# Keeping the residual rows of a small hybrid network unscaled between its blocks, with both norm factors from one chain of roots

## The chip, the cores and the metric
One core of a Trainium2 chip runs one program. Its engines are TensorE (PE in the profile, with its weight loads as PEld), VectorE (DVE), ScalarE (ACT), GpSimd (POOL) and SyncE (SP, which here only issues transfers). The metric is device time in microseconds (us); lower is better. Quoted times are the median of several runs, and a trace is one profiled execution.

## The reference, cut to what matters
The network takes x of 512 tokens by 1024 features through a first block and two hybrid layers. The first block ends in a residual sum and a norm, and its result is both the residual and, after one more norm, the input of the first layer:

```python
x = x + jnp.einsum('bse,ed->bsd', y, w_out[layer])
return _rmsnorm(x, final_norm_g)              # end of the first block
...
h = rms_norm(x, norm1_g)                      # start of a hybrid layer
...
x = x + merged.astype(dt) @ w_out
h2 = rms_norm(x, norm2_g)                     # then the feed-forward part
```

With s the unnormed sum, the first norm is s times r1 times gf1 (r1 a factor per token, gf1 a gain per feature). The second norm needs the squares of that product.

## The kernel before, in words
Activations lie feature-major: eight tiles [128 features, 512 tokens]. Every product is made of three float32r matmuls (`mm3`, lines 387 to 391: high by high, low by high, high by low). A weight chunk is loaded by SP (line 376), its high part is cast by ACT (line 382) or, each fourth, by DVE (line 380), and its low part is the difference, on DVE (line 383). Two buffers each of the raw, high and low chunk rotate. A chunk is one projection of 24 matmuls with 512 columns (`proj`), or a third of a token-major product (`proj_tm`, lines 420 to 422, tiles named pt).

The framework orders the instructions of each engine ahead of time, by its own estimate of their times (`schedule_with_timeline_sim=True`). At run time each engine works in that order, and an instruction that must wait holds up what stands behind it on its engine.

**End of the first block** (`block1`, lines 652 to 684). For m from 0 to 7: load a piece of the input into x0 (tag f, three buffers, SP), project, add on DVE into X[:, m, :] (line 665), make the next layer's operand hh and hl with the gains gf1*g1 (`gained`, lines 507 and 509), and collect two sums of squares on ACT and POOL (`sq_add`, lines 494 to 501). Behind the loop, `col_rstd` sums each over the partitions with eight one-column matmuls (line 470), and `rsqrt` takes a root by a first guess and three Newton steps on DVE, on [128, 4] values (lines 451 to 460). The second root needs the first (`rows=r1`). Their product rc is spread to [128, 512] by four transposes (`spread`, line 486) and copied to Rsb (`rows`, line 523). Then r1 is spread as well and copied to R1 (line 675).

**Scaling the rows.** `late()` multiplies each X[:, k, :] by gf1 on ACT (line 681) and by R1 on POOL (line 682). It is called by `keep()`, the first job (`room`) of the next layer, which then writes all of X to DRAM in one transfer from ACT's queue (line 1067). The buffer of X is then taken over by M, which collects the four branches. For the second layer `late` does nothing, and the one transfer is made.

**Start of a layer.** The first jobs of `mlstm` are a token-major product `av(0)` of three chunks (816, 816 and 544 columns; its results go through lines 1276, 1225, 1226, 1230), then q and k projections with a convolution (`pre`: lines 530, 1289, 1290, 1292, 1296) and the gates' rows (`gates`, lines 1394 to 1412).

**End of the branches** (`layer`, lines 1072 to 1086). M, complete after the last adds on POOL (line 1193), is split into mh and ml (lines 437 and 438). Then for m from 0 to 7: load x0 from DRAM (line 1082), project, add on DVE (line 1084), make hh and hl, and add the squares.

**The last products of a layer** (lines 1106 to 1118) add into X[:, m, :] and make the next operand.

Of the kernel before, what the change touches and what calls it, by code (L numbers as in the profile page):

```python
# [8 lines left out]
F32 = mybir.dt.float32  # L9
F32R = mybir.dt.float32r  # L10
I32 = mybir.dt.int32
AF = mybir.ActivationFunctionType
ALU = mybir.AluOpType
# [14 lines left out]
# ---------------------------------------------------------------- layout  # L28
# Every weight matrix is cut into chunks [K, n]; a chunk is stored as
# [128 partitions, K/128, n], and the chunks follow one another in one array.  # L30
# [231 lines left out]
# buffers of each tag; pj, S, T and O share the eight banks of PSUM  # L262
BUFS = dict(a=5, c=3, f=3, b=4, y=4, P=6, qs=2, ks=2, ph=2, vx=2, wr=2, wh=2, wl=2, pj=3, S=2, T=2,
            O=1)
# the tag that each small product or transpose takes its bank from
# [8 lines left out]
# ---------------------------------------------------------------- kernel  # L274


class Net:
# [16 lines left out]
    # ---- small helpers  # L294
# [39 lines left out]
    def load(self, dst, src):  # L334
        """behind the input"""
        with self.tc.issue_after(self.last):
            self.nc.sync.dma_start(dst, src)
# [32 lines left out]
    # ---- weights: load, then split w = hi + lo exactly  # L370
# [22 lines left out]
    def proj(self, key, h, tag="pj", w=None, n=P):  # L393
        """feature-major: out[n, tok] = sum_k w[k, n] h[k, tok]"""
# [8 lines left out]
    def proj_tm(self, key, h, evac, tags=("pj", "pj")):  # L403
        """token-major: out[tok, n] for 4 blocks of 128 tokens, as many to a bank as fit"""
# [22 lines left out]
    def split(self, hi, lo, src, scale=None, hi_eng=None, lo_eng=None):  # L427
        """src (times a power of two) = hi + lo exactly, both float32r"""
# [12 lines left out]
    def rsqrt(self, r, ms, scale, rows=None):  # L441
        """r = (ms * rows^2 * scale + eps)^-1/2 of a few columns: a first guess from the exponent,
        three steps of Newton's iteration"""
        v = self.nc.vector
        shape = [P, r.shape[1]]
        x, t = self.small(shape, "rx"), self.small(shape, "rt")
# [7 lines left out]
        v.tensor_scalar(out=x, in0=ms, scalar1=scale, scalar2=EPS, op0=ALU.mult, op1=ALU.add)  # L454
        v.tensor_scalar(out=r.bitcast(I32), in0=x.bitcast(I32), scalar1=-0.5, scalar2=float(0x5F3759DF),
# [5 lines left out]

    def col_rstd(self, sqs, n, w=1, rows=None, tag="st"):
        """(sum over features of squares / n * rows^2 + eps)^-1/2 with tokens on partitions:
        [128, 4 * w]; w = 2: one for each half of the features"""
# [11 lines left out]
    def spread(self, r, w=1, tag="R"):  # L476
        """[tok, 4 * w] to feature-major [128, 512]"""
# [11 lines left out]
    def sq_add(self, acc, k, x, parts=1, scale=1.0):  # L489
        """collect the squares of scale * x over the tiles of a row; parts = 2: the last on its own"""  # L490
# [12 lines left out]
    def gained(self, h, k, x, gain, lo_eng=None):  # L503
        """x * gain as hi and lo. The products of a norm take x * gain as it is; what comes out of
        them is scaled by the row's factor: self.R feature-major, self.rc with tokens on partitions"""
# [13 lines left out]
    def rows(self, rc):  # L519
        """set the factors of a norm"""  # L520
        self.rc = rc
        self.R = self.cp.tile([P, S], F32, tag="R", name="Rsb")
        self.nc.vector.tensor_copy(self.R, self.spread(rc))

    def scaled(self, ps, scale=1.0, out=None):
        """a projection times the factors of its norm"""
# [8 lines left out]
    def twice_silu(self, ps, out):  # L535
        """2 silu(z) = (1 + tanh(z/2)) z, z = ps * R"""
# [7 lines left out]
    def log_sigmoid(self, x, shape):  # L544
        """min(x, 0) - log1p(exp(-|x|)), log1p(u) = 2 atanh(u / (2 + u)) as a series"""
# [24 lines left out]
    # ---- heads of 64: [hi; lo] stacks fill the 128 rows, so two products carry all four parts  # L570
    def stack_q(self, dst, src):
        """dst[:, 0]: even head as [hi; lo]; dst[:, 1]: odd head as [lo; hi]"""
# [4 lines left out]
    def stack_k(self, dst, src):  # L577
        """dst[:, 0:2] as stack_q; dst[:, 2:4] with the halves exchanged"""
# [6 lines left out]
    def heads_v(self, v, b, o, n):  # L585
        """v[:, head, 0:64] hi, v[:, head, 64:128] lo from o [tok, n*64] of token block b"""
# [7 lines left out]
    def softmax_rows(self, pt, src, nmax, n, scale=1.0):  # L594
        """pt = exp(scale src - max) / sum along the free axis"""
# [15 lines left out]
    def y_out64(self, O, y, par):  # L611
        """y rows of this head = O[0:64] + O[64:128]"""
# [5 lines left out]
    # ---------------------------------------------------------------- first block  # L618
    def block1(self):
# [20 lines left out]
        with tc.tile_pool(name="yp", bufs=1) as yp:  # L640
# [5 lines left out]
            with tc.tile_pool(name="fx", bufs=1, reuse_waits="tile") as fx:  # L646
# [3 lines left out]
                # the final norm of this block and the first norm of the next layer together: both  # L650
                # sums of squares are taken before the first factor is known
# [6 lines left out]
                acc, acc2 = [], []  # L658
                for m in range(8):
# [5 lines left out]
                    nc.vector.tensor_tensor(out=x, in0=ps, in1=x0, op=ALU.add)  # L665
                    self.gained(h, m, x, gg[:, m:m + 1])
                    self.sq_add(acc, m, x)
                    self.sq_add(acc2, m, x, scale=self.prm("gf1", m))
        r1 = self.col_rstd(acc, D)
        r2 = self.col_rstd(acc2, D, rows=r1)  # L670
        rc = self.small([P, 4], "rc", 1)
        nc.vector.tensor_tensor(out=rc, in0=r1, in1=r2, op=ALU.mult)
        self.rows(rc)
        R1 = self.ftmp("R1")
        nc.scalar.copy(R1, self.spread(r1))

        def late():
            """the rows of this block as the next layer adds them"""
            for k in range(8):
                x = X[:, k, :]  # L680
                nc.scalar.activation(x, x, AF.Copy, scale=self.prm("gf1", k))
                nc.gpsimd.tensor_tensor(out=x, in0=x, in1=R1, op=ALU.mult)

        return X, h, late
# [376 lines left out]
    def layer(self, l, X, h, late):  # L1061
# [3 lines left out]
        def keep():  # L1065
            late()
            nc.scalar.dma_start(xs, X)
# [710 lines left out]
```

## Time and profile before
| | |
|---|---|
| time, median of 3 runs | 2515.54 us (2514.5 to 2517.31) |
| span of the profiled execution | 2516.1 us |
| PE busy | 2478.7 us, 99% |
| PEld, DVE, ACT, POOL busy | 82%, 66%, 39%, 23% |
| chain that ended last | PE 92%, DVE 5%, issue 1%, ACT 1%, POOL 1% |
| transfers | 232.09 MB, mean 92 GB/s |

The profiled execution has no time of its own beside its span; the span lies 0.56 us above the median of the runs and within their spread. Busy time of PE contains modelled ends of matmuls, so it says where PE waited and not how well it was used. Beside the busy times stands PE's granted clock: 1.00 is its upper level of 2.4 GHz, 0.50 its lower level of 1.2 GHz.

### The profile page before, as it was taken

How to read it: one execution, taken by the hardware profiler on the slowest of the kernel's cores; microseconds unless marked ns; L12 is line 12 of the kernel's file. 1: busy time of each engine (PE TensorE's matmuls, PEld its weight loads, DVE VectorE, ACT ScalarE, POOL GpSimd, SP SyncE). 2: the span in 40 equal slices, each digit the busy share in tenths (PEclk: the TensorE clock that was granted, in tenths of full speed). 3: DMA queues.
4: the chain of work that ended last, by engine and by line, in shares of the span. 5: the costliest groups of instructions: out<-in, count | busy, mean ns of one | idle time of the engine just before them, and what ended most of it. 6: DMA issues, size and time to landing. Idle time of an engine off the chain costs nothing.

```text
span 2516.1 us, 32999 instructions
## 1 busy us (share of the span) xinstructions
PE 2478.7 (99%) x12256; PEld 2058.2 (82%) x12256; DVE 1650.3 (66%) x3313; ACT 973.8 (39%) x1714; POOL 569.3 (23%) x612
## 2 busy tenths in 40 slices
PE   8999999999999999999999999999999999999998
PEld 6778778888888888788888888888888888888886
DVE  7956589878778754554344488697788655543543
ACT  5324454444555532322122344445555323221221
POOL 4612163313132111211011133131421112110111
PEclk9989999999999999999999999999999999999999
DMA  4211232223233222322322322222322223223222
GB/s 151 68 62 60 76 122 94 74 72 93 73 104 95 85 86 96 128 92 88 105 101 88 131 85 70 76 89 76 104 87 93 74 94 126 99 87 108 92 94 91
DMA packets 71168, 232.09 MB, mean 92 GB/s; under 512 B 8256, under 2 KB 10832, under 8 KB 70752
## 3 DMA queue, kind: packets, MB, share of 16 engines
q1 hardware_dynamic: 66848, 213.90, 25.1%
q10 hardware_dynamic: 4096, 15.99, 2.3%
q8 instruction: 96, 1.57, 0.3%
q0 software_dynamic: 64, 0.10, 0.1%
q14 instruction: 64, 0.52, 0.1%
HBM read 212.14 MB, written 6.29 MB: 87 GB/s over the span
## 4 chain that ended last, share of the span: by engine, by line
PE 92%; DVE 5%; issue 1%; ACT 1%; POOL 1%; DMA 0%; SPq 0%; DVEq 0%; POOLq 0%; ACTq 0%
PE pj L391 14%; PE pj L389 14%; PE pj L390 14%; PE S L391 4%; PE S L389 4%; PE S L390 4%; PE dn L389 3%; PE dn L391 3%; PE dn L390 3%; PE up L389 2%; PE up L391 2%; PE up L390 2%; PE pt L421 2%; PE pt L420 2%; PE pt L422 2%; PE st L470 1%
## 5 line engine op out<-in xcount | busy, mean ns | idle before, releaser
L391 PE MATMUL pj<-hh,wl 128*128 128x512 f32 x1632 | 644.9, 395 | 4.3 <-DVE wl L383 4.2
L389 PE MATMUL pj<-hh,wh 128*128 128x512 f32 x1632 | 645.3, 395 | 0.4 <-DVE og L530 0.4
L390 PE MATMUL pj<-hl,wh 128*128 128x512 f32 x1632 | 643.6, 394 | 0.0
L382 ACT CAST wh<-wr 128x1024 fp32r<-128x1024 f32 (+3 forms) x296 | 296.1, 1001 | 770.0 <-PE pj L390 294.1
L383 DVE TENSOR_TENSOR wl<-wr,wh 128x1024 fp32r<-128x1024 f32 (+3 forms) x397 | 479.8, 1209 | 127.6 <-ACT wh L382 123.8
L391 PEld LDWEIGHTS pj<-hh,wl 128*128 128x128 f32 x1632 | 308.2, 189 | 71.1 <-DVE wl L383 7.4
L390 PEld LDWEIGHTS pj<-hl,wh 128*128 128x128 f32 x1632 | 308.1, 189 | 62.2
L389 PEld LDWEIGHTS pj<-hh,wh 128*128 128x128 f32 x1632 | 308.1, 189 | 61.8 <-DVE og L530 0.6
L600 POOL TENSOR_SCALAR P<-P,l 128x512 f32<-128x512 f32 (+3 forms) x160 | 102.2, 643 | 434.3 <-DVE l L599 334.3
L1096 POOL TENSOR_TENSOR pr<-pr,Rsb 128x512 f32<-128x512 f32 x44 | 73.1, 1663 | 514.9 <-ACT th L1095 514.9
L389 PE MATMUL S<-hh,wh 128*128 128x512 f32 x368 | 144.4, 392 | 7.3 <-DVE wh L380 7.3
L380 DVE CAST wh<-wr 128x1024 fp32r<-128x1024 f32 (+4 forms) x101 | 70.2, 695 | 122.8 <-PE pj L390 62.7
L391 PE MATMUL S<-hh,wl 128*128 128x512 f32 x368 | 144.3, 392 | 2.2 <-DVE wl L383 2.2
L390 PE MATMUL S<-hl,wh 128*128 128x512 f32 x368 | 144.2, 392 | 0.0
L607 ACT CAST ph<-T 128x512 fp32r<-128x512 f32 x192 | 103.4, 561 | 102.2 <-PE T L1477 34.2
L1193 POOL TENSOR_TENSOR M<-M,gt 128x512 f32<-128x512 f32 x48 | 74.0, 1542 | 299.3 <-DVE gt L1191 244.5
L389 PE MATMUL dn<-ah,wh 128*128 128x512 f32 x352 | 137.0, 389 | 0.0
L390 PE MATMUL dn<-al,wh 128*128 128x512 f32 x352 | 137.0, 389 | 0.0
L391 PE MATMUL dn<-ah,wl 128*128 128x512 f32 x352 | 137.0, 389 | 0.0
L608 DVE TENSOR_TENSOR pl<-T,ph 128x512 fp32r<-128x512 f32 x192 | 122.4, 649 | 19.9 <-ACT ph L607 18.3
L421 PE MATMUL pt<-wl,hh 128*128 128x256 f32 (+2 forms) x384 | 110.0, 288 | 2.2 <-DVE wl L383 2.2
L530 DVE TENSOR_TENSOR pr<-pj,Rsb 128x512 f32<-128x512 f32 x74 | 50.7, 687 | 92.8 <-PE pj L391 92.3
(430 smaller groups left out, 4676.8 us busy)
## 6 DMA issues: line engine op xcount, KB each, us to landing
wr<-in_wall_dram SPq DMA_DIRECT2D x324, 512.0 KB, 3.5
wr<-in_wall_dram SPq DMA_DIRECT2D x32, 384.0 KB, 3.0
ks<-ks ACTq DMA_DIRECT2D x44, 256.0 KB, 3.7
wr<-in_wall_dram SPq DMA_DIRECT2D x32, 320.0 KB, 2.9
xs<-X ACTq DMA_DIRECT2D x2, 2048.0 KB
x<-xs SPq DMA_DIRECT2D x16, 256.0 KB, 2.7
strip<-in_rp_dram SPq DMA_DIRECT2D x16, 192.0 KB
X<-in_xT_dram SPq DMA_DIRECT2D x8, 256.0 KB, 6.8
```

Of the source, the lines that this page charges most:

```text
L380: nc.vector.tensor_copy(wh[:, 0:e], raw[:, 0:e])
L382: nc.scalar.copy(wh[:, 0:e], raw[:, 0:e])
L383: nc.vector.tensor_tensor(out=wl[:, 0:e], in0=raw[:, 0:e], in1=fv(wh[:, 0:e]), op=ALU.subtract)
L389: mm(out, wh, xh, start=start, stop=False)
L390: mm(out, wh, xl, start=False, stop=False)
L391: mm(out, wl, xh, start=False, stop=stop)
L421: mm(o[b], xh, wl, start=False, stop=False)
L600: nc.gpsimd.tensor_scalar(out=pt[:, 0:n], in0=pt[:, 0:n], scalar1=l, scalar2=1.0, op0=ALU.mult, op1=ALU.mult)
L607: nc.scalar.copy(th[:, 0:n], T[:, 0:n])
L608: nc.vector.tensor_tensor(out=tl[:, 0:n], in0=T[:, 0:n], in1=fv(th[:, 0:n]), op=ALU.subtract)
L1096: nc.gpsimd.tensor_tensor(out=z, in0=z, in1=self.R, op=ALU.mult)
L1193: nc.gpsimd.tensor_tensor(out=M[:, m, :], in0=M[:, m, :], in1=t, op=ALU.add)
```

## The change
1. `two_rstd` takes the place of two `col_rstd` calls. The 16 one-column matmuls go into one bank; x[:, 0:4] = S1/n + eps and x[:, 4:8] = (x[:, 0:4] * eps * n + S2)/n are formed, and one Newton chain on [128, 8] gives r1 and at once the product rc of both factors.
2. `late`, `keep` and the one large transfer of each layer are gone. Each piece X[:, m, :] is written to DRAM from ACT's queue right behind its add: unscaled at the end of the first block, as it is at the end of the first layer.
3. R1 is still spread and copied, and is now written to DRAM (r1s, 256 KB).
4. Where the first layer loads x0, `normed` reads R1 back once (SP's queue, tag c) and scales each x0 by gf1 on ACT and by R1 on POOL, ahead of the DVE add.

The rest of the diff takes out comments. Its core:

```diff
     def rsqrt(self, r, ms, scale, rows=None):
...
         v.tensor_scalar(out=x, in0=ms, scalar1=scale, scalar2=EPS, op0=ALU.mult, op1=ALU.add)
+        self.newton(r, x)
+
+    def newton(self, r, x):
+        v = self.nc.vector
+        t = self.small([P, r.shape[1]], "rt")
         v.tensor_scalar(out=r.bitcast(I32), in0=x.bitcast(I32), scalar1=-0.5, scalar2=float(0x5F3759DF),
                         op0=ALU.mult, op1=ALU.add)
...
+    def two_rstd(self, acc, acc2, n):
+        nc, v = self.nc, self.nc.vector
+        st = self.psum(BANK["st"], "st")
+        for i, sq in enumerate((acc, acc2)):
+            for b in range(4):
+                nc.tensor.matmul(st[:, 4 * i + b:4 * i + b + 1], sq[:, P * b:P * b + P], self.ones,
+                                 start=i == 0 and b == 0, stop=i == 1 and b == 3)
+        x, r = self.small([P, 8], "x2", 1), self.small([P, 8], "rr", 1)
+        v.tensor_scalar(out=x[:, 0:4], in0=st[:, 0:4], scalar1=1.0 / n, scalar2=EPS, op0=ALU.mult, op1=ALU.add)
+        v.scalar_tensor_tensor(out=x[:, 4:8], in0=x[:, 0:4], scalar=EPS * n, in1=st[:, 4:8],
+                               op0=ALU.mult, op1=ALU.add)
+        v.tensor_scalar(out=x[:, 4:8], in0=x[:, 4:8], scalar1=1.0 / n, scalar2=None, op0=ALU.mult)
+        self.newton(r, x)
+        return r[:, 0:4], r[:, 4:8]
...
                 acc, acc2 = [], []
+                xs = self.rows_kept()
                 for m in range(8):
...
                     nc.vector.tensor_tensor(out=x, in0=ps, in1=x0, op=ALU.add)
+                    nc.scalar.dma_start(xs[:, m, :], x)
                     self.gained(h, m, x, gg[:, m:m + 1])
...
-        r1 = self.col_rstd(acc, D)
-        r2 = self.col_rstd(acc2, D, rows=r1)
-        rc = self.small([P, 4], "rc", 1)
-        nc.vector.tensor_tensor(out=rc, in0=r1, in1=r2, op=ALU.mult)
+        r1, rc = self.two_rstd(acc[0], acc2[0], D)
         self.rows(rc)
         R1 = self.ftmp("R1")
         nc.scalar.copy(R1, self.spread(r1))
-        def late():
-            for k in range(8):
-                x = X[:, k, :]
-                nc.scalar.activation(x, x, AF.Copy, scale=self.prm("gf1", k))
-                nc.gpsimd.tensor_tensor(out=x, in0=x, in1=R1, op=ALU.mult)
-        return X, h, late
+        r1s = self.dp.tile([P, S], F32, name="r1s")
+        nc.scalar.dma_start(r1s, R1)
+        st = {}
+        def normed(x, k):
+            if not st:
+                st["R1"] = self.tmp("R1", "c")
+                nc.sync.dma_start(st["R1"], r1s)
+            nc.scalar.activation(x, x, AF.Copy, scale=self.prm("gf1", k))
+            nc.gpsimd.tensor_tensor(out=x, in0=x, in1=st["R1"], op=ALU.mult)
+        return xs, h, normed
...
-    def layer(self, l, X, h, late):
+    def layer(self, l, xs, h, normed):
...
-        def keep():
-            late()
-            nc.scalar.dma_start(xs, X)
...
                 nc.sync.dma_start(x0, xs[:, m, :])
+                if normed:
+                    normed(x0, m)
                 ps = self.proj(("wo", l, m), (mh, ml), ("S", "T")[m % 2])
...
                     if half:
                         if more:
+                            nc.scalar.dma_start(xs[:, m, :], X[:, m, :])
                             self.gained(h, m, X[:, m, :], self.prm(("g1", l + 1), m))
...
                 def room():
-                    keep()
                     M.append(self.big.tile([P, 8, S], F32, tag="X", name="M"))
```

## Rows read from the trace of the kernel before
**Rows 1.** The page's first part, with busy time, share of the span and instructions of each engine.
```profile
PE 2478.7 (99%) x12256; PEld 2058.2 (82%) x12256; DVE 1650.3 (66%) x3313; ACT 973.8 (39%) x1714; POOL 569.3 (23%) x612
```
**Rows 2.** The windows view of the start of the first layer: length, busy time of PE, PEld, DVE, ACT and POOL, granted clock, DMA share, GB/s.
```profile
355.50:360.50 5.00, 2.81 (x23) 2.60 (x22) 4.15 (x4) 1.26 (x2) 4.98 (x4) 1.00 0.00 0
360.50:366.00 5.50, 3.15 (x23) 2.72 (x23) 5.50 (x5) 1.56 (x2) 5.50 (x4) 1.00 0.26 95
366.00:370.00 4.00, 4.00 (x11) 3.13 (x12) 4.00 (x10) 1.42 (x3) 3.98 (x3) 0.57 0.39 131
```
**Rows 3.** The timeline of PE there: start, us, instruction, and in brackets the idle time before it with its releaser.
```profile
346.58 1.84 PE L470 MATMUL st<-ones,acc 128*128 128x1 f32 x16
...
355.16 0.40 PE L420 MATMUL pt<-wh,hh 128*128 128x272 f32 x1 [0.34 <-DVE Rsb L523]
...
357.53 0.66 PE L420 MATMUL pt<-wh,hh 128*128 128x272 f32 x4
360.37 0.40 PE L421 MATMUL pt<-wl,hh 128*128 128x272 f32 x1 [2.19 <-DVE wl L383]
...
365.97 0.50 PE L391 MATMUL pj<-hh,wl 128*128 128x512 f32 x1 [2.35 <-DVE wl L383]
...
369.95 0.39 PE L389 MATMUL pj<-hh,wh 128*128 128x512 f32 x1
370.18 0.39 PE L390 MATMUL pj<-hl,wh 128*128 128x512 f32 x1
```
**Rows 4.** The timeline of DVE there, in the same columns.
```profile
348.13 0.15 DVE L454 TENSOR_SCALAR rx<-st 128x4 f32<-128x4 f32 x1
...
352.94 0.16 DVE L672 TENSOR_TENSOR rc<-r,r 128x4 f32<-128x4 f32 x1
354.42 0.69 DVE L523 COPY Rsb<-R 128x512 f32<-128x512 f32 x1 [1.32 <-PE R L486]
...
356.76 1.86 DVE L1290 SCALAR_TENSOR_TENSOR cv<-pr,prm_t,cv 128x511 f32<-128x511 f32 x1 [0.85 <-ACT cv L1289]
358.54 1.78 DVE L383 TENSOR_TENSOR wl<-wr,wh 128x544 fp32r<-128x544 f32 x1
360.24 1.77 DVE L380 CAST wh<-wr 128x1024 fp32r<-128x1024 f32 x1
361.93 1.78 DVE L1292 SCALAR_TENSOR_TENSOR cv<-pr,prm_t,cv 128x511 f32<-128x511 f32 x1
363.63 2.29 DVE L383 TENSOR_TENSOR wl<-wr,wh 128x1024 fp32r<-128x1024 f32 x1
```
**Rows 5.** The timeline of POOL there.
```profile
355.52 13.21 POOL L682 TENSOR_TENSOR X<-X,R 128x512 f32<-128x512 f32 x8 [9.67 <-ACT R L675]
```
**Rows 6.** The timeline of DVE at the same place of the second layer.
```profile
1439.89 0.72 DVE L383 TENSOR_TENSOR wl<-wr,wh 128x544 fp32r<-128x544 f32 x1 [0.32 <-ACT wh L382]
1440.53 0.74 DVE L1290 SCALAR_TENSOR_TENSOR cv<-pr,prm_t,cv 128x511 f32<-128x511 f32 x1
...
1441.98 1.22 DVE L383 TENSOR_TENSOR wl<-wr,wh 128x1024 fp32r<-128x1024 f32 x1
```
**Rows 7.** The windows view of stretches of both layers (columns as in rows 2): PE's idle is the length less the first busy time.
```profile
370.00:400.00 30.00, 29.64 (x133) 24.24 (x132) 29.14 (x53) 13.95 (x25) 5.33 (x6) 1.00 0.44 158
...
1010.00:1020.00 10.00, 9.08 (x40) 7.14 (x38) 8.10 (x10) 5.34 (x9) 1.84 (x2) 1.00 0.22 79
1020.00:1030.00 10.00, 9.60 (x42) 7.98 (x43) 5.63 (x7) 1.52 (x2) 1.60 (x1) 1.00 0.50 159
...
1440.00:1460.00 20.00, 20.00 (x101) 17.03 (x100) 19.90 (x47) 11.64 (x24) 4.03 (x5) 1.00 0.38 132
1460.00:1500.00 40.00, 38.81 (x175) 31.30 (x174) 33.73 (x59) 15.91 (x27) 8.68 (x16) 1.00 0.24 79
1500.00:2100.00 600.00, 598.96 (x3056) 501.83 (x3055) 449.51 (x1071) 279.34 (x529) 146.86 (x193) 1.00 0.26 85
```
**Rows 8.** The timeline of DVE where the first layer's output projections begin and run.
```profile
1018.04 2.30 DVE L383 TENSOR_TENSOR wl<-wr,wh 128x1024 fp32r<-128x1024 f32 x1
...
1022.07 2.30 DVE L383 TENSOR_TENSOR wl<-wr,wh 128x1024 fp32r<-128x1024 f32 x1
...
1037.72 1.23 DVE L383 TENSOR_TENSOR wl<-wr,wh 128x1024 fp32r<-128x1024 f32 x1 [0.21 <-ACT wh L382]
```
**Rows 9.** The timeline of POOL there: the last two adds of the branches.
```profile
1017.65 1.61 POOL L1193 TENSOR_TENSOR M<-M,gt 128x512 f32<-128x512 f32 x1 [7.42 <-DVE gt L1191]
1021.69 1.60 POOL L1193 TENSOR_TENSOR M<-M,gt 128x512 f32<-128x512 f32 x1 [2.42 <-DVE gt L1191]
```
**Rows 10.** The timeline of ACT there: a cast that waits until PE has finished with the chunk whose buffer it takes.
```profile
1036.64 1.05 ACT L382 CAST wh<-wr 128x1024 fp32r<-128x1024 f32 x1 [2.67 <-PE S L390]
```
**Rows 11.** DVE's instructions grouped by line, 316 to 345 us (end of the first block, POOL adding squares beside them): busy time, mean ns.
```profile
L509 DVE SCALAR_TENSOR_TENSOR hl<-X,gg,hh 128x512 fp32r<-128x512 f32 x8 | 12.5, 1579 | 0.0
L665 DVE TENSOR_TENSOR X<-pj,x 128x512 f32<-128x512 f32 x2 | 1.4, 680 | 0.0
```
**Rows 12.** All instructions of line 681: duration in ns (least, median, most), first and last start.
```profile
L681 ACT ACTIVATE X<-X,prm_t x8: 707/725/727, 321.7 to 343.5; 128x512 f32<-128x512 f32 x8
```
**Rows 13.** The page's part on transfers: the loads of the residual rows, KB each and us to landing.
```profile
x<-xs SPq DMA_DIRECT2D x16, 256.0 KB, 2.7
```
**Rows 14.** All instructions on the tile M, its first writer in the layers: duration in ns, first and last start.
```profile
L530 DVE TENSOR_TENSOR M<-pj,Rsb x16: 675/690/693, 491.1 to 1617.8; 128x512 f32<-128x512 f32 x16
```

More of the change, by code (lines that the diff above doesn't have):

```diff
@@ L445, in rsqrt @@
         shape = [P, r.shape[1]]
-        x, t = self.small(shape, "rx"), self.small(shape, "rt")
+        x = self.small(shape, "rx")
         if rows is not None:
@@ L675, in block1, with rows_kept @@
         nc.scalar.copy(R1, self.spread(r1))
-        def late():
-            for k in range(8):
-                x = X[:, k, :]
-                nc.scalar.activation(x, x, AF.Copy, scale=self.prm("gf1", k))
-                nc.gpsimd.tensor_tensor(out=x, in0=x, in1=R1, op=ALU.mult)
-        return X, h, late
+        r1s = self.dp.tile([P, S], F32, name="r1s")
[8 more added lines that the diff above has]
+        return xs, h, normed
+    def rows_kept(self):
+        self.nk = getattr(self, "nk", -1) + 1
+        return self.dp.tile([P, 8, S], F32, name="xs%d" % self.nk)
     def y_pair(self, pool):
@@ L1058, in pv64 @@
             mm(O[0:64], v[:, 0:64], tl, start=False, stop=False)
-    def layer(self, l, X, h, late):
+    def layer(self, l, xs, h, normed):
         nc, tc, v = self.nc, self.tc, self.nc.vector
-        xs = self.dp.tile([P, 8, S], F32, name="xs%d" % l)
-        def keep():
-            late()
-            nc.scalar.dma_start(xs, X)
         with tc.tile_pool(name="al%d" % l, bufs=1, reuse_waits="tile") as ap:
             self.ap = ap
-            M = self.branches(l, h, keep)
+            M = self.branches(l, h)
             mh = self.big.tile([P, 8, S], F32R, tag="A", name="mh", bufs=2)
@@ L1105, in layer @@
                         h = self.pair(self.big, "A", 2)
+                        xs = self.rows_kept()
                 for m in range(8):
@@ L1121, in layer, with branches @@
                 self.rows(R)
-        return (X, h, lambda: None) if more else (X, R)
-    def branches(self, l, h, keep):
+        return (xs, h, None) if more else (X, R)
+    def branches(self, l, h):
         mk = (self.mlstm, self.gqa, self.natten, self.diff)
```

## The prediction
> **What bounds the kernel now.** I read the page's first part first: PE is busy for 2478.7 us of the span of 2516.1 [rows 1]. So all that PE ever waits is 37.4 us, and a change that leaves its matmuls alone can win only from that, or from a stretch at the lower clock. I then asked the windows view where these waits lie. Beside the start and the end of the program, which the change does not touch, the largest group is the start of the first layer. There PE is idle for 2.19 us of 355.5 to 360.5 and for 2.35 us of 360.5 to 366, and from 366 to 370 it is busy throughout at a granted clock of 0.57 [rows 2]. DVE is nearly full in all three stretches and POOL is full.
>
> The timelines say why. PE waits 0.34 us for Rsb, 2.19 us and 2.35 us for low parts of weight chunks [rows 3], and both low parts come late from DVE [rows 4]. There a difference of 544 columns takes 1.78 us; the same one at the start of the second layer takes 0.72 us [rows 4, 6]. The convolution step at line 1290 takes 1.86 us against 0.74, and a difference of 1024 columns 2.29 against 1.22 [rows 4, 6]. What the first layer has and the second has not is the eight POOL multiplies by R1, one behind the other from 355.52 us for 13.21 us [rows 5]. So the bound of this stretch is DVE, made late by a chain of two roots and slowed by `late` beside it, and then PE at its lower clock behind the two waits.
>
> **The change part by part.**
>
> *One chain of roots.* Before: 11 instructions for the first root, 13 for the second (two multiplies by r1 more) and the product, 25 in all, from 348.13 to 353.10 us [rows 4], 0.20 us each. After: three to form x and ten of Newton, 13, so 2.6 us on [128, 8], which I price as [128, 4]. It begins when all 16 one-column matmuls are done, at 348.42 [rows 3], 0.3 us later than now. It ends at about 351.05, 2.05 us earlier. By itself this is worth at most the 2.05 us, and only while DVE is the bound.
>
> *`late` taken out of the start.* The wait at 360.37 is gone if the low part of 544 columns is ready when PE comes to it. By the old order: Rsb starts 2.05 us earlier, at 352.4, and the same steps lead to line 1290 at 354.7 (356.76 less 2.05). With the second layer's durations, 0.74 and 0.72, the low part is ready at 356.2. PE reaches it at 357.85: it ended its other matmuls at 358.2 [rows 3], less the 0.34 us for Rsb, if that goes too. So there is 1.6 us to spare. The next: cast at most 1.77 as now (nearer 0.7), convolution 0.74, difference 1.22 give 359.9 at most; PE comes to it 3.25 us (365.97 less 2.35 less 360.37) after 357.85, at 361.1. Both waits go. The multiplies themselves were hidden otherwise: M's first writer in the layers starts at 491.1 us [rows 14], long behind.
>
> *The lower clock.* From 365.97 to 369.95 PE starts ten matmuls 0.40 us apart; at the upper clock they are 0.23 us apart [rows 3]. That is 1.7 us. The fall follows the two waits, so it goes with them; the second layer starts at a clock of 1.00 [rows 7].
>
> Together 0.34 + 2.19 + 2.35 + 1.7 = 6.6 us. What is late next is the gates' chain of scans at the layer's start: 0.36 us of waiting in the first layer, 1.19 us in the second [rows 7], where nothing had gone wrong before it. The first layer may come to look like the second, which costs 0 to 0.83 us more; I take 0.4, the middle, as neither row is nearer.
>
> *`normed` at the output projections.* Eight ACT scalings of 0.72 us [rows 12] and eight POOL multiplies (13.21 / 8 = 1.65 us each [rows 5]) move here, with one more load of 256 KB on SP's queue. ACT and POOL have room. Queued behind the new waits: on SP, behind the load of R1, the other x0 and weight loads (its buffer of tag c is free by then, so it only costs the issue); on ACT, behind a scaling that waits for its x0, the casts; on POOL, behind a multiply, the last adds into M and the squares. Steady state is safe: a cast waits for PE to leave its buffer at 1036.64, its low part is done at 1038.95 [rows 8, 10], and PE needs it one projection after it left the buffer, 24 steps of 0.23 or 5.5 us, which leaves about 3.2 us. An x0 goes through its load of 2.7 us [rows 13], 0.72 and 1.65, some 5 us, and three buffers give it 16. The start is not safe: PE waits there already, 0.92 and 0.40 us [rows 7], for a low part that took 2.30 instead of 1.22 us beside a POOL add, and the next one is slowed in the same way [rows 8, 9]. The multiplies for pieces 0 and 1 can fall there. Nothing before shows this place with them: between no cost and 8 x 1.08 = 8.6 us (every multiply delaying a needed low part by 2.30 less 1.22), with a gain of 1.3 possible, should another order remove today's wait. I take 0.9: most of one such delay, as only the first two pieces can meet the tight part.
>
> Here the Trainium skill speaks against the change. At the end of the first block the step hl, with two operands from SBUF, takes 1579 ns beside POOL's additions, while the add with an operand from PSUM stays at 680 [rows 11]. "SBUF — State Buffer" (section on ports) says that GpSimd and VectorE take a shared pair of ports as an exclusive lock, and that the later one blocks fully. The rows agree. By that rule the eight multiplies keep their price wherever they stand.
>
> *Pieces to DRAM.* Two transfers of 2 MB become 16 of 256 KB on ACT's queue, plus R1. An issue on ACT waits for the add that hh behind it waits for as well, so no new wait stands before hh; in the first block it takes the place of a longer scaling of 0.72 us [rows 12]. PE is fully busy where the second layer begins [rows 7], so nothing is to be won there, and I cost this at nothing. The cover is PE's lead of one chunk; if it is gone, a late load costs up to 2.7 us [rows 13].
>
> *Order elsewhere.* The framework orders all instructions anew. The same layer is ordered twice in this kernel: behind its start and the gates, the waits sum to 1.3 us in one (1010 to 1030 us) and 1.0 us in the other (1500 to 2100 us) [rows 7]. A new order should therefore move the rest by under 1 us.
>
> Sum: -6.6 + 0.4 + 0.9 = -5.3 us. Against the span of 2516.1 this is 2510.8; the span lies 0.56 us above the median of the runs, 2515.54, so the forecast in the terms of the median is 2510.2. A measurement of this kernel tells some 0.2%, 5 us, from no change; the forecast stands almost on that border.
>
> **The rivals.**
>
> 1. *The lock moves with the work.* If the first multiplies meet the chain of mh, ml and low parts in the output projections, three or four of them delay PE by 1.08 us each, 3.2 to 4.3 in place of the 0.9 of the sum: 2512.5 to 2513.6. For it: both low parts at that place are slowed already. Against it: the steady margin of 3.2 us. The rule above is this rival's ground.
> 2. *The waits only half go.* If the new order puts the difference of 544 columns behind other DVE work, one of the two waits (2.2 us) stays and with it most of the lost clock (1.7): 2510.2 + 3, about 2513. For it: DVE is busy 29.14 of 30 us behind the stretch [rows 7]. Against it: over 1 us to spare at both places.
> 3. *More goes.* The wait of 1.3 us at the output projections is ordered away, the multiplies find room and the gates' chain is not late: 2515.5 - 6.6 - 1.3, about 2507.6.
> 4. *Slower than before.* The multiplies stand on PE's path: each DVE add waits for its x0, the bank of its projection is held, and PE stops in every one of the eight projections. Eight times 1.65 us is 13.2 us, less 6.6 won, so 2522. It decides once the loop of add, load, scaling, multiply and next add passes three projections, 16 us; its parts sum to 5 us, so queueing would have to add 11. Little speaks for it.
> 5. *No effect.* The other engines were slow for another reason and nothing moves: 2515.5. The second layer's start speaks against it.
>
> **How the numbers follow.** Forecast, with its own spread from 2508.6 to 2512: 0.57. Rival 1: 0.17. Rival 2: 0.10. Rival 3: 0.09. Rival 4: 0.05. Rival 5: 0.02. Faster by over 0.2% means below 2510.5: some 0.4 of the forecast's 0.57 and all of rival 3, so 0.49. Slower by over 0.2% is rival 4 alone, 0.05. The rest, 0.46, lies within 0.2%. The range runs from rival 3 with half a microsecond for another order, 2507.0, to rivals 1 and 2 with about one, 2514.2.
>
> **What would show it.** Right: between 350 and 372 us of the new profile no POOL work beside DVE but one split, 13 small DVE instructions between the sums and Rsb, the difference of 544 columns near 0.72 us, PE without waits over 0.5 us and at a clock of 1.00. ACT scalings and POOL multiplies lie at about 1010 to 1060 us, and PE's wait at 1020 has grown by about 1 us. Wrong: a wait of PE for a low part at the layer's start in spite of short DVE steps (rival 2), several waits between 1010 and 1030 (rival 1), or a wait for a bank in each output projection (rival 4). The scans' waits in both layers show whether the 0.4 us was right. If the waits go and the time does not follow, something outside these two places was ordered worse.

## The result and the profile after

| | before | after |
|---|---|---|
| time, median | 2515.44 us (4 runs) | 2538.05 us (2536.69 to 2539.39, 4 runs) |
| ratio, 95% interval | | 1.0088 [1.0075, 1.0101] |
| span of the profiled execution | 2516.1 us | 2537.7 us |

The change makes the kernel 0.9% slower. The forecast was 2510.2 us in a range from 2507.0 to 2514.2, so it is wrong in its sign and the time lies outside its range.

The page's first part of the kernel after answers to [rows 1]; the second line is from its part on transfers:

```profile
PE 2505.1 (99%) x12256; PEld 2058.5 (81%) x12256; DVE 1650.6 (65%) x3301; ACT 974.8 (38%) x1714; POOL 570.2 (22%) x612
...
xs<-X ACTq DMA_DIRECT2D x16, 256.0 KB, 3.5
```

PE has the same 12256 instructions and is busy for 26.4 us longer, and PE waits less: 2537.7 less 2505.1 is 32.6 us, against 37.4. No other engine has more to do worth naming, and the mean granted clock is 0.992 against 0.993. So the loss is not a wait, and not the clock. Before looking for it, the place that the prediction was about. The windows view of the start of the first layer, after (columns as in [rows 2]; the kernel has come here about 2.6 us later than before):

```profile
350.00:360.00 10.00, 9.65 (x78) 9.41 (x78) 5.13 (x17) 1.85 (x3) 0.00 (x0) 1.00 0.23 79
360.00:370.00 10.00, 9.99 (x56) 8.64 (x55) 9.85 (x26) 5.66 (x14) 2.58 (x3) 1.00 0.48 159
370.00:400.00 30.00, 29.65 (x134) 24.19 (x134) 29.10 (x46) 13.48 (x21) 5.16 (x5) 1.00 0.27 88
1440.00:1500.00 60.00, 58.81 (x306) 50.20 (x305) 49.75 (x93) 27.99 (x50) 10.89 (x16) 1.00 0.27 88
```

The waits of 2.19 and 2.35 us and the clock of 0.57 of [rows 2, 3] are gone: PE is idle for 0.36 us of the first 20 us and the clock is 1.00 throughout. POOL does nothing from 350 to 360, where it was full. The timeline of DVE there, after, answers to [rows 4]:

```profile
351.45 0.16 DVE L477 TENSOR_SCALAR x<-st 128x4 f32<-128x4 f32 x1 [0.50 <-PE st L474]
...
353.87 0.17 DVE L465 SCALAR_TENSOR_TENSOR rr<-rt,rr 128x8 f32<-128x8 f32 x1
357.03 0.69 DVE L545 COPY Rsb<-R 128x512 f32<-128x512 f32 x1 [3.00 <-PE R L508]
...
359.37 0.75 DVE L1316 SCALAR_TENSOR_TENSOR cv<-pr,prm_t,cv 128x511 f32<-128x511 f32 x1 [0.85 <-ACT cv L1315]
360.04 0.72 DVE L383 TENSOR_TENSOR wl<-wr,wh 128x544 fp32r<-128x544 f32 x1
360.68 0.69 DVE L380 CAST wh<-wr 128x1024 fp32r<-128x1024 f32 x1
361.28 0.74 DVE L1318 SCALAR_TENSOR_TENSOR cv<-pr,prm_t,cv 128x511 f32<-128x511 f32 x1
361.94 1.22 DVE L383 TENSOR_TENSOR wl<-wr,wh 128x1024 fp32r<-128x1024 f32 x1
```

The steps that took 1.86, 1.78, 1.77, 1.78 and 2.29 us in [rows 4] take 0.75, 0.72, 0.69, 0.74 and 1.22, the durations of the second layer in [rows 6]. The chain of roots has 13 instructions in 2.6 us, as forecast, but Rsb follows it 3.00 us later, where it came 1.32 us behind rc [rows 4]. The timeline of PE, after, says why:

```profile
356.28 0.28 PE L422 MATMUL pt<-wh,hl 128*128 128x272 f32 x1
356.40 1.03 PE L508 MATMUL R<-cst,rr 128*128 128x128 f32 x8
```

PE works without a pause up to the transposes that spread the factors, and they stand behind other products in its order. They did not wait for the roots.

Now the whole span, in stages that are bounded by the first matmul of a kind in the timeline of PE. The third column is experiment e5, the same change with its tiles placed as before:

| stage | before | after | e5 |
|---|---|---|---|
| program start to the first block's output projections | 302.5 | 305.1 | 302.2 |
| to the gates' maxima of the first layer (the forecast's 6.2 us) | 99.0 | 92.6 | 92.5 |
| rest of the branches of the first layer | 617.0 | 618.8 | 616.9 |
| output projections of the first layer | 50.1 | 50.6 | 50.5 |
| feed-forward part of the first layer, with the start of the second | 413.7 | 424.0 | 413.7 |
| rest of the branches of the second layer | 614.0 | 616.2 | 614.1 |
| output projections of the second layer | 49.4 | 49.5 | 49.5 |
| feed-forward part of the second layer, to the end | 370.4 | 380.9 | 370.5 |

The gain is there, 6.4 us. The two feed-forward parts, which the change touches in no line but one write of a row, lose 10.3 and 10.5 us, the branches 1.8 and 2.2. (The first row varies from 300.3 to 305.1 us over all kernels of this study, and by 2 us among those with the tiles placed as before, 300.3 to 302.5, so its difference is not read here.) In the feed-forward part PE never pauses; the windows view of 300 us of it, before:

```profile
1100.00:1400.00 300.00, 300.00 (x1325) 248.53 (x1324) 137.13 (x173) 71.04 (x93) 37.22 (x22) 1.00 0.29 95
```

and after:

```profile
1100.00:1400.00 300.00, 300.00 (x1287) 240.99 (x1286) 132.55 (x167) 68.99 (x90) 35.97 (x21) 1.00 0.30 96
```

PE is busy for 300.00 of 300 us at a clock of 1.00 in both, with the same transfers beside it, but finishes 1287 matmuls in place of 1325. The reader is to look at the count, since the busy time can't show it. Taken from the starts in the timeline, the mean step from one matmul to the next is 226.7 ns before and 233.3 after, at each of the lines 389, 390 and 391 within 0.4. The feed-forward parts have 352 matmuls of the tile dn at each of these three lines and twice as many for the other products, 3168 in all; times 6.6 ns this is 20.9 us, and the table's two rows lose 20.8.

### The profile page after: what moved, and what is told of

It reads as the page before. It is cut to its first block, busy times and chain, and to the rows that moved or that the text cites. A ratio compares the mean times of both kernels' runs of the same rounds, so it can differ in the third digit from the quotient of the medians.

```text
span 2537.7 us, 33031 instructions
## 1 busy us (share of the span) xinstructions
PE 2505.1 (99%) x12256; PEld 2058.5 (81%) x12256; DVE 1650.6 (65%) x3301; ACT 974.8 (38%) x1714; POOL 570.2 (22%) x612
## 4 chain that ended last, share of the span: by engine, by line
PE 92%; DVE 5%; issue 1%; ACT 1%; POOL 1%; DMA 0%; SPq 0%; DVEq 0%; POOLq 0%; ACTq 0%
PE pj L391 14%; PE pj L389 14%; PE pj L390 14%; PE S L391 4%; PE S L389 4%; PE S L390 4%; PE dn L390 3%; PE dn L389 3%; PE dn L391 3%; PE up L389 2%; PE up L390 2%; PE up L391 2%; PE pt L421 2%; PE pt L420 2%; PE pt L422 2%; PE st L492 1%
## 5 line engine op out<-in xcount | busy, mean ns | idle before, releaser
L552 DVE TENSOR_TENSOR pr<-pj,Rsb 128x512 f32<-128x512 f32 x74 | 50.6, 687 | 97.7 <-PE pj L391 97.3
```

## The experiments

**The theories.** The new [128, 8] tiles x2 and rr take 32 bytes of each partition each, and rc, which goes, took 32 as well (its values fill 16; that e2 has the steps of after and e5 those of before bears this out); so every pool that is opened behind them starts 32 bytes later in SBUF. The operands of the feed-forward products (hh, hl, ah, al) lie in such pools. The weight buffers, the split M and the operand of the branches do not. Theory A: where the operands lie sets the step of the matmuls (A1: by their own address; A2: by their distance to the weights). Theory B, the rival: the change's work slows PE, by the new order, the writes of pieces, or the scalings beside it. In the kernels that only add an unused tile (e1 to e4, e9 to e12), each engine's instructions stand in the order of the kernel that they were made from, and those of e5 in the order of the kernel after. Each ratio is to runs of the kernel before on the same chip, with medians from 2516.6 to 2517.3 us.

The windows view of the same 300 us is shown for most; the count behind PE's busy time is what to read. Steps are means from one matmul's start to the next over these 300 us of the first layer's feed-forward part, some 430 to 440 at each of the lines 389, 390 and 391; steps above 300 ns (a wait, or a missing record) are left out.

**e1: after, and 32 unused bytes behind its small tiles.** Everything opened later starts 64 bytes further than before the change.

```diff
-        x, r = self.small([P, 8], "x2", 1), self.small([P, 8], "rr", 1)
+        x, r = self.small([P, 8], "x2", 1), self.small([P, 8], "rr", 1); self.small([P, 8], "pad", 1)
```

> The changed kernel with one unused tile of 32 bytes per partition behind the small tiles, so that all pools opened later lie 32 bytes higher; every engine's instructions and their order stay the same. In the changed kernel these pools had moved up by 32 bytes against the kernel before, and matmuls whose streamed operand lies in them start 233.4 ns apart instead of 226.6. Theory A (start address): the step goes back to 226.6 to 227 in the feed-forward parts, some 3,170 matmuls by 6.8 ns or 21.5 us, and 2 to 3 us more in the branches come back: 2512 to 2516. Rival B (the new order, the 16 transfers or the read of R1 slow TensorE): nothing moves, 2538 with steps of 233.

2520.75 us, ratio to before 1.0014 [1.0005, 1.0023]; steps 231.7, 225.8 and 229.2, mean 228.9.

```profile
1100.00:1400.00 300.00, 300.00 (x1312) 246.16 (x1311) 135.43 (x171) 69.76 (x92) 37.30 (x22) 1.00 0.31 98
```

An unused tile wins back most of the loss. That is for theory A, but the steps are not those of before and the time lies above the 2512 to 2516 expected by it, so a distance of 64 bytes is better than 32 and not as good as none.

**e2: before, and 32 unused bytes.** Nothing of the change is in it.

```diff
-        rc = self.small([P, 4], "rc", 1)
+        rc = self.small([P, 4], "rc", 1); self.small([P, 8], "pad", 1)
```

> The kernel before with the same unused tile of 32 bytes, nothing else changed; its later pools then start where those of the changed kernel start. Theory A: steps of 233 ns in the feed-forward parts and 2537 to 2541 us. Rival B: 2515.5 with steps of 227.

2543.36 us, ratio 1.0108 [1.0093, 1.0123]; steps 233.4, 233.2 and 233.4.

```profile
1100.00:1400.00 300.00, 300.00 (x1287) 241.02 (x1286) 134.62 (x168) 69.44 (x91) 35.07 (x21) 1.00 0.29 92
```

The kernel before becomes as slow in this stage as the one after, 1287 matmuls in 300 us. Theory B can't explain this: no work was added.

**e3 and e9: after, with 64 and 96 unused bytes** (`[P, 16]` and `[P, 24]` in e1's edit; 96 and 128 bytes further than before).

> The changed kernel with an unused tile of 64 bytes in place of 32. Theory A with a period of 64 bytes: the streamed rows start at a multiple of 64 again, steps of 233 and 2536 to 2540 us. With a period of 128 bytes or more: anything else, a step between 226 and 234 that the first run does not have. Rival B: 2538, which does not tell it from the period of 64, but the first run does.

> The changed kernel with an unused tile of 96 bytes, order of all instructions the same: the streamed operands of the layers now stand 128 bytes further from the weights than in the kernel before. So far distances of 32, 64 and 96 bytes more gave steps (mean over the three matmuls of a group) of 233.3, 228.9 and 233.3 ns against 226.7. If the pattern has a period of 128 bytes: 226.7 again and the time of e5, about 6 us below the kernel before (ratio 0.9975). If each added 32 bytes only draws another value: a step between 229 and 238, 2520 us or more.

e3: 2536.22 us, 1.0077 [1.0063, 1.0091], steps 237.4, 231.0 and 231.6, mean 233.3. e9: 2532.54 us, 1.0060 [1.0045, 1.0075], steps 233.0, 233.4 and 233.6, mean 233.3. Neither 64 bytes (e1) nor 128 (e9) bring back 226.7, so the period is neither of the two. In the second layer's feed-forward part, where the tiles lie at the same distances, e3 has 231.0, 231.5 and 237.4: the longest step has moved from line 389 to line 391, and the mean has stayed. So the mean of the three says what a placement costs, and one line's step doesn't say which product is hit. For e9 the mean there is 232.4.

**e4: after, and 32 unused bytes ahead of all other tiles.** The operands lie where they lie in e1, and the weights 32 bytes further as well, so their distance is that of the kernel after.

```diff
-        self.ones = cp.tile([P, 1], F32, name="ones")
+        self.ones = cp.tile([P, 1], F32, name="ones"); cp.tile([P, 8], F32, name="pad")
```

> The changed kernel with the unused 32 bytes at the very front, so that constants, weight buffers and every other tile move up by 32 bytes: the weights now start at a multiple of 64, the operands of the branches' projections too, those of the feed-forward parts 32 past one. It tells two forms of theory A apart by the steps, not by the time. A1 (the start of the streamed operand alone decides): feed-forward steps of 227, branch projections and output projections slower than before, towards 233. A2 (its distance from the start of the weights decides): feed-forward steps stay at 233, branch projections stay as they were, 2538. Rival B: no step changes, 2538.

2537.29 us, 1.0079 [1.0065, 1.0093]; steps 233.4, 233.2 and 233.4.

```profile
1100.00:1400.00 300.00, 300.00 (x1288) 240.98 (x1287) 133.14 (x166) 68.99 (x90) 35.91 (x21) 1.00 0.30 94
```

The same operand address as in e1, and 233.3 in place of 228.9: A1 falls, A2 stands.

**e5: after, with the tiles of the layers where they were.** The roots' x goes into the tile rx, which is there anyway, and the place of rc goes to rr.

```diff
-        x, r = self.small([P, 8], "x2", 1), self.small([P, 8], "rr", 1)
+        x, r = self.small([P, 8], "rx"), self.small([P, 8], "rr", 1)
```

> The changed kernel with x of two_rstd in the old small tile rx instead of one of its own. That takes back the 32 bytes, and every tile of the layers stands where it stood in the kernel before; order of all instructions as in the changed kernel. Distance theory (the step of a matmul depends on the distance between the starts of its streamed operand and of the weights): steps of 226.6 everywhere, and only the effects that the prediction had worked out are left, 6.4 us less before the gates' maxima and 0.4 us more at the output projections: 6 us below the kernel before, ratio 0.9975. If something else of the change costs time as well: ratio 1.000 or above.

2511.65 us (11 runs), before 2516.76 on the same chip; ratio 0.9979 [0.9970, 0.9988]; steps 226.9, 226.3 and 226.8.

```profile
1100.00:1400.00 300.00, 300.00 (x1326) 248.47 (x1325) 136.99 (x172) 71.91 (x95) 37.14 (x23) 1.00 0.32 101
```

All of the change's work is in it and none of the loss. It beats both kernels.

**e6: the roots alone.** The kernel before with `two_rstd` (x in rx), `late` and the large transfers kept.

```diff
-        r1 = self.col_rstd(acc, D)
-        r2 = self.col_rstd(acc2, D, rows=r1)
-        rc = self.small([P, 4], "rc", 1)
-        nc.vector.tensor_tensor(out=rc, in0=r1, in1=r2, op=ALU.mult)
+        r1, rc = self.two_rstd(acc[0], acc2[0], D)
```

> The kernel before with two_rstd alone (x in rx, so no tile moves); late and the one large transfer stay. Prediction's reading: the eight POOL multiplies still delay DVE at the start of the layer, so most of the waits stay and only the 2 us of the shorter chain come off: 1 to 2.5 us faster, the difference of 544 columns still 1.7 us or longer. Rival (the chain of roots was the whole cause): 6 us faster.

2516.94 us, 1.0002 [0.9993, 1.0011]: no gain. The timeline of POOL in it:

```profile
353.76 13.23 POOL L706 TENSOR_TENSOR X<-X,R 128x512 f32<-128x512 f32 x8 [9.68 <-ACT R L699]
```

of DVE:

```profile
352.66 0.69 DVE L550 COPY Rsb<-R 128x512 f32<-128x512 f32 x1 [3.38 <-PE R L513]
...
356.78 1.78 DVE L383 TENSOR_TENSOR wl<-wr,wh 128x544 fp32r<-128x544 f32 x1
```

and what PE waited for from 340 to 400 us:

```profile
PE pj L391 <- DVE wl L383: 2.7, 2, 2.4
PE pt L421 <- DVE wl L383: 2.2, 1, 2.2
PE pt L420 <- DVE Rsb L550: 0.3, 1, 0.3
```

This kernel runs 1.8 us ahead of before from its first block on: the one-column matmuls start at 344.83 in place of 346.58 [rows 3]. From there to Rsb it takes 7.83 us (352.66 less 344.83), against 7.84 before (354.42 less 346.58 [rows 3, 4]). The shorter chain is followed by a longer wait for the transposes. The multiplies start as early behind Rsb as they did, and the slow steps and waits of [rows 2 to 4] are back, with a granted clock of 0.72 from 364 to 370 us. The 1 to 2.5 us that were expected of the roots did not come.

**e7: the rows alone.** The kernel after, with the two old chains and rc; e6's edit the other way round.

> The changed kernel with the two old chains of roots, so the rows' part alone; no tile moves. Prediction's reading: without POOL beside it DVE makes the low part of 544 columns 2.2 us sooner than before, which covers the wait of 2.19 us almost exactly, the second wait and the lower clock go: 4 to 6.5 us faster. Rival (the chain of roots was the cause): no more than 2 us faster.

2512.43 us, 0.9982 [0.9973, 0.9991]. The timeline of DVE, with its low part of 544 columns:

```profile
352.13 0.69 DVE L545 COPY Rsb<-R 128x512 f32<-128x512 f32 x1 [1.19 <-PE R L508]
...
355.13 0.72 DVE L383 TENSOR_TENSOR wl<-wr,wh 128x544 fp32r<-128x544 f32 x1
```

and what PE waited for from 340 to 400 us:

```profile
PE pj L391 <- DVE wl L383: 0.4, 1, 0.4
PE pt L420 <- DVE Rsb L545: 0.3, 1, 0.3
```

The gain of the change is that of the rows' part: the stage to the gates' maxima takes 92.5 us here as in e5, 99.1 in e6, 99.0 before.

**e8: e5 without the scaling of the rows.** `normed(x0, m)` is replaced by `pass`, so this kernel leaves out the two factors on the residual rows of the first layer.

> The kernel of e5 without normed: the first layer adds the rows unscaled and does not read R1, so eight ACT scalings, eight POOL multiplies and one load of 256 KB are left out. It measures what they cost at the output projections: by the prediction 0.9 us, by the trace of the changed kernel 0.4 us, by rival 1 of the prediction 3 to 4 us. Expected 0 to 1 us faster than e5.

2511.86 us, 0.9979 [0.9970, 0.9988], no difference from e5 that the runs can tell. What is left stands in the order of e5. In the profiles the output projections of the first layer take 49.1 us in place of 50.5, and PE's wait there (990 to 1100 us) is

```profile
PE S L391 <- DVE wl L383: 0.2, 1, 0.2
```

in place of 1.3 in e5. The scalings have a price of about 1.4 us, which is below what whole runs resolve.

**e10 and e11: before, with 32 bytes inside the weights' pool.** In e10 they lie behind the high and low weight buffers, so that the operands of all products move away from the weights; in e11 between the high and the low buffers.

```diff
# e10
+        self.nw += 1; self.nw == 1 and self.wp.tile([P, 8], F32, tag="pad", name="pad", bufs=1)
# e11: the same tile, made after wh and before wl
```

> The kernel before with the unused 32 bytes directly behind the weight buffers, so that weights stay and all later tiles move, the operands of the branches' and output projections too. Distance theory: the steps of the output projections rise from 226.6 to 233 as well (384 matmuls per layer), those of the branches' projections from their mean of 229 by up to 5, the feed-forward steps to 233 as in e2: 2543 + 5 + 10 to 20, so 2555 to 2570 on a chip with 2517 before. If only the feed-forward and later pools matter: 2543, output projections at 227.

> The kernel before with the unused 32 bytes between the high and the low weight buffers: the low weights keep their distance to the streamed operands, the high weights stand 32 bytes off. It asks which weights count for a step, those that the running matmul holds or those that are loaded for the next one while it streams. Own weights: steps behind L389 and L390 (both on the high weights) 233, behind L391 227. Weights being loaded for the next: steps behind L389 and L391 (the next one takes high weights) 233, behind L390 (the next one takes low weights) 227. Either way some two thirds of the cost: about 2517 + 15 to 28. No dependence on weights at all: all steps alike.

e10: 2554.15 us, 1.0148 [1.0133, 1.0163], just under the 2555 to 2570 expected by the distance theory. The mean step is now 233.3 in the output projections of the first layer too (227.5 before), and 233.0 in the projections of its branches (229.1 before). The windows view of 25 us of the output projections, before:

```profile
1035.00:1060.00 25.00, 25.00 (x112) 20.68 (x111) 12.03 (x15) 9.44 (x14) 7.49 (x5) 1.00 0.42 140
```

and in e10:

```profile
1035.00:1060.00 25.00, 25.00 (x108) 19.91 (x108) 13.22 (x16) 10.02 (x14) 5.92 (x4) 1.00 0.49 151
```

So the rule holds for other operands, in other stages. In e10 the operands keep their distance to all tiles behind the weights, so it is the distance to the weights' pool or to the constants ahead of it that counts.

e11: 2555.0 us, 1.0146 [1.0129, 1.0163], steps 236.0, 233.2 and 230.8 in the feed-forward part, mean 233.3. That is as slow as e10, where some two thirds of the cost were expected, and it fits neither reading: by a product's own weights the step behind line 391 would have stayed, by the weights loaded for the next one that behind line 390. All three are longer, and e3 shows that a long step can change lines, so which read of which buffer meets which stays open.

**e12: after, with the operands 256 and 512 bytes further than before.** 224 unused bytes behind the small tiles move hh and hl by 256 bytes, and a tile of 256 bytes behind them moves ah and al by 512.

```diff
+        x, r = self.small([P, 8], "x2", 1), self.small([P, 8], "rr", 1); self.small([P, 56], "pad", 1)
...
+            h = self.pair(fp); fp.tile([P, 64], F32, name="pad")
```

> The changed kernel with two unused tiles, the order of all instructions the same: hh and hl of the feed-forward parts stand 256 bytes further from the weights than in the kernel before, ah and al 512 bytes. Shifts of 32, 96 and 128 gave a mean step of 233.3 ns, 64 gave 228.9, none gave 226.7. If the pattern has a period of 256 bytes: 226.7 in both groups, about 2511 on a chip with 2517 before. Period of 512: 226.7 for the products of ah and al alone. No period up to 512: neither.

2512.02 us, 0.9983 [0.9973, 0.9992]; steps 226.9, 226.3 and 226.8; the mean is 226.8 for hh and 226.7 for ah.

```profile
1100.00:1400.00 300.00, 300.00 (x1326) 248.39 (x1325) 136.99 (x173) 72.29 (x95) 36.73 (x22) 1.00 0.31 100
```

Both places are as good as that of before. All shifts together (mean step of the three lines in the first layer, and the kernel's ratio to before):

| shift against the weights, bytes | 0 (e5) | 32 (after) | 64 (e1) | 96 (e3) | 128 (e9) | 256 and 512 (e12) |
|---|---|---|---|---|---|---|
| step, ns | 226.7 | 233.3 | 228.9 | 233.3 | 233.3 | 226.7 |
| ratio | 0.9979 | 1.0088 | 1.0014 | 1.0077 | 1.0060 | 0.9983 |

This fits a period of 256 bytes, which only two shifts, 256 and 512, bear out. Shifts of 160, 192 and 224 were not tried.

## Why the prediction was wrong

**The step that failed** is "Order elsewhere": "A new order should therefore move the rest by under 1 us." The rest moved by some 27 us: after against e5 is 1.0088 against 0.9979, 1.1% of 2515, and e2 loses 26.1 us (2543.36 less 2517.26) by 32 unused bytes alone. The prediction asked for waits that a new order could bring, and found rightly that there would be few: in e5, with the new order and the old places, the rest of the branches and the feed-forward parts differ from before by 0.1 us at most. It took the pace of a matmul for a constant of the kernel. The change's small tiles were priced by the instructions on them, at 0.20 us each; that a new tile moves all that is placed behind it was in no term, and none of the five rivals had it. Rival 4, the slower one, needed PE to stop in each output projection; it doesn't, in any profile. The last sign of the prediction, waits that go and a time that does not follow, came true, but not as it was read there: nothing was ordered worse, the same matmuls ran slower.

The other terms, one by one:

- **The two waits and the clock: right.** 2.19, 2.35 and 1.7 us are gone, by the mechanism given (the multiplies leave DVE's side: e7 against e6). By the rule of the Trainium skill ("SBUF — State Buffer", section "SBUF: two separate sides"), a DVE step with two SBUF inputs and a GpSimd step that reads SBUF hold a shared pair of ports one after the other. The runs agree: the low part of 544 columns takes 1.78 us beside the multiplies in e6, and 0.72 without them in e7.
- **The wait of 0.34 us for Rsb: stays** at 0.3 us, with the short chain and with the long one. That Rsb comes 2.05 us earlier failed: by PE's order the transposes start 2.4 us behind the chain's end, and Rsb comes 3.00 us behind it. From the one-column matmuls to Rsb it takes 7.58 us after and 7.58 in e7 with the two old chains. Before, too, PE worked without a pause up to the transposes, which start 0.68 us behind rc:

```profile
353.78 0.60 PE L486 MATMUL R<-cst,rc 128*128 128x128 f32 x4
```

  So the prediction's reading that the chain of two roots made DVE late was wrong: without the second chain Rsb comes as late in e6. The mistake cost nothing, since the slow steps went for the other reason.
- **The gates' chain: 0.4 us forecast, none measured.** PE is idle for 0.35 us from 370 to 400 us after, 0.36 before, and for 1.19 us in the second layer in both [rows 7].
- With these the stage was to win 6.2 us, and won 6.4 (99.0 to 92.6).
- **`normed`: 0.9 us forecast, 0.4 to 0.5 measured** (50.1 to 50.6, and 50.5 in e5). The multiplies fall on the tight place as feared; the timeline of POOL, after:

```profile
1015.60 1.61 POOL L1219 TENSOR_TENSOR M<-M,gt 128x512 f32<-128x512 f32 x1 [7.41 <-ACT gt L1204]
1017.17 2.26 POOL L707 TENSOR_TENSOR x<-x,R 128x512 f32<-128x512 f32 x1
1020.67 1.67 POOL L1219 TENSOR_TENSOR M<-M,gt 128x512 f32<-128x512 f32 x1 [1.23 <-DVE gt L1217]
1022.30 2.26 POOL L707 TENSOR_TENSOR x<-x,R 128x512 f32<-128x512 f32 x1
```

  and of DVE beside it:

```profile
1015.98 2.32 DVE L383 TENSOR_TENSOR wl<-wr,wh 128x1024 fp32r<-128x1024 f32 x1
...
1021.11 2.31 DVE L383 TENSOR_TENSOR wl<-wr,wh 128x1024 fp32r<-128x1024 f32 x1
```

  But both low parts were as slow before (2.30 us beside the adds into M [rows 8, 9]), so they lose nothing more, and PE's wait is 1.2 us (1.3 before). Without the scalings the new order would have won 1.0 us here (49.1 in e8 against 50.1); they cost 1.4 of that back. Rivals 1 and 3 each held in part and nearly cancelled.
- **Pieces to DRAM: nothing forecast, nothing seen.** The 16 writes land in 3.5 us and no wait of PE names them.

Without the loss the sum would have been right: e5's ratio of 0.9979 on the time before, 2515.44, is 2510.2 us, with an interval from 2507.9 to 2512.4. That it meets the forecast to the tenth is luck: by the two profiles e5 wins 6.5 us at the layer's start and gives back 0.4 at the output projections, 6.1 us against 5.3 forecast, and the runs don't resolve that difference.

## What to carry to other kernels

When a change adds or drops a tile, of any size, compare the start-to-start step of the matmuls it does not touch, by counting them in a window where PE never pauses: busy time hides a slower pace. If the step has moved, try the change with its tiles in the place of old ones, or with an unused tile that brings back the old step (here one that made the shift 256 or 512 bytes), before judging it. And a shorter chain wins nothing while the instruction that uses its result stands behind full work in another engine's order: look up that place before pricing the chain.

## What the runs showed of the hardware

The pace of these float32r matmuls of 512 columns, each with its own weight load, at a granted clock of 1.00 with no wait, depends on the distance in SBUF between the streamed operand and the weight buffers: 226.7 ns from start to start (mean over the three products) at one distance and at 256 and 512 bytes more, 233.3 at 32, 96 and 128 more (232.4 at 128 more in the second layer), 228.9 at 64 more. Over the 3168 matmuls of the feed-forward parts the worst of these costs 21 us, and where the projections of the branches move too, the kernel loses 1.5% (e10). It is the distance and not the address of the operand (e1 against e4).

Other engines and transfers are not needed for it. In the 300 us of the windows view, the traces have 41 steps after and 31 before with no instruction of DVE, ACT or POOL and no transfer packet within 0.2 us of them; their means are 233.2 and 226.6 ns. That two reads of SBUF for PE meet in the same part of the memory would give such a picture, but this is only argued: no run told apart which reads they are, and e11, which moved the low weights against the high ones, slowed all three products.
